# A depthwise convolution of 31 taps: one channel tile on TensorE as diagonal products, or two as 32x32 products

## The chip, the cores and the metric

The kernel runs on one core of one Trainium2 chip. The metric is the device time of one execution in microseconds (us); the median of three runs stands for a kernel. On the core five engines work side by side, each through its own queue in order: TensorE (PE: products; PEld: its weight loads), VectorE (DVE), ScalarE (ACT), GpSimd (POOL) and SyncE (SP, which issues the DMA transfers). TensorE multiplies a stationary block, contracted over up to 128 partitions, with a moving block and adds into banks of PSUM, 128 partitions by 512 values of f32; the other engines read these banks out.

## What is computed

Two layers of a decoder over 256 positions of 1024 channels. Layer 0 has attention and a feed-forward part, layer 1 a gated mixer with a convolution, and again a feed-forward part. The change lies in the convolution of layer 1:

```python
def odd_mixer(h, w_in, b_in, w_out, ln_g, ln_b, w_s, b_s, conv_w, conv_b, cln_g, cln_b):
    proj = h @ w_in + b_in
    gz, ca, cg = jnp.split(proj, [2 * GMLP_WIDTH, 2 * GMLP_WIDTH + CONV_CH], axis=-1)
    gu, gv = jnp.split(jax.nn.gelu(gz), 2, axis=-1)
    ...
    c_out = gu * sg.reshape(B, S, GMLP_WIDTH)
    c = ca * jax.nn.sigmoid(cg)
    c = lax.conv_general_dilated(c, conv_w[:, None, :], window_strides=(1,),
                                 padding=[(CONV_KERNEL - 1, 0)], ...
                                 feature_group_count=CONV_CH) + conv_b
    d_out = jax.nn.silu(layer_norm(c, cln_g, cln_b))
    return jnp.concatenate([c_out, d_out], axis=-1) @ w_out
```

The convolution is depthwise: each of 512 channels has 31 weights of its own, and its output at a position is the weighted sum of the channel at that position and the 30 before it. `sg` is a causal product over blocks of 128 positions, the gate of the other half of the mixer.

## The kernel before, in words

All large products run on TensorE in a split form: an operand is kept as a rounded part (hi) and a remainder (lo), both of type FR, and a product is three passes, hi by hi, lo by hi and hi by lo (`passes`, L222 to L228). Weights come in blocks of 1 MB through three load buffers; ScalarE makes hi (L131), VectorE or GpSimd makes lo (L135), into eight buffers each. These splits are put into a list and taken from it at every `PACE`-th tick, a tick being counted for each 256 columns of a product (L180 to L187).

TensorE's order is the order of the code. GpSimd's is too in the stretch of the change (`pool_order`, L1137), and VectorE's from L1241 on. ScalarE's order, and VectorE's before L1241, are set by a scheduler that may move an operation ahead of others that come before it in the code; on the chip each engine then works its queue strictly in that order.

In layer 1, channels lie on partitions and positions along the row; there are four channel tiles (ct) of 128. The order on TensorE is:

1. `gated(0)`, half of gv, `gated(1)` (L1091): the products for `ca` and `cg`; ScalarE takes the sigmoid, VectorE writes the gated channels with 30 zeros ahead into `cpad`.
2. `project_gu(0)` (L1112), 12 taps of the convolution of tile 3, `project_gu(1)`.
3. The gate, `spatial(p)` for p = 0 to 3 (L1122), with two taps of tile 3 behind each: four small f32 products on 64 columns of the array; ScalarE copies the result out (L1131), GpSimd adds and multiplies (L1132, L1133), ScalarE rounds (L1134), GpSimd takes the remainder (L1135).
4. The other 11 taps of tile 3.
5. The output projection (`out_steps`, L1213), 16 steps of three passes of 512 columns, into four banks taken at that point. Between the steps, in the numbers of `SOME`, stand the small products of the layer norm: `mean` (L1170), the variance (L1188), the scale (L1198). Behind the 16 steps follow those on the convolution's own outputs, which need the norm's result.

Tile 3 is convolved on TensorE (`taps_pe`, L1056): a tap is a product with a diagonal matrix that holds the tap's weight of each channel. A diagonal exists in hi and lo, so a tap is three passes of 256 columns. The 62 diagonals are made by ScalarE from the identity (`tap_diag`, L926), 24 of them in layer 0's feed-forward part and 38 in stage 1. Tiles 0 to 2 are convolved on VectorE (`tap_dve`, L1068): a tap is one operation that multiplies a shifted row of `cpad` with a weight and adds an accumulator in PSUM (`cacc`). These are issued with the ticks, `TAP_RATE` of one per tick, and what is left behind the last product.

Products take a bank from a pool of four (`mm_bank`), used in turn. `tq` in this stretch is a single bank, and `cacc` three more, one for each tile that VectorE convolves.

## Time and profile before

| what | us |
|---|---|
| median of three runs | 617.0 (616.12 to 617.19) |
| the profiled execution's own time | 616.31 |
| its span, first to last instruction | 614.6 |
| TensorE busy in the span | 600.3 (98%) |
| VectorE busy | 409.7 (67%) |
| ScalarE busy | 345.9 (56%) |
| GpSimd busy | 96.7 (16%) |

The rows that follow behind the change are from this one execution. Times in a row are us from the start of the span. In an order of time the columns are: start, duration, engine, line, operation, tile written <- tiles read, shape, count; in square brackets the idle time before it and who ended it. A product's duration includes its way through the array, so products overlap in the rows; the pace is the distance of their starts. A product of two f32 operands shows as two passes.

### The profile page before, as it was taken

How to read it: one execution, taken by the hardware profiler on the slowest of the kernel's cores; microseconds unless marked ns; L12 is line 12 of the kernel's file. 1: busy time of each engine (PE TensorE's matmuls, PEld its weight loads, DVE VectorE, ACT ScalarE, POOL GpSimd, SP SyncE). 2: the span in 40 equal slices, each digit the busy share in tenths (PEclk: the TensorE clock that was granted, in tenths of full speed). 3: DMA queues.
4: the chain of work that ended last, by engine and by line, in shares of the span. 5: the costliest groups of instructions: out<-in, count | busy, mean ns of one | idle time of the engine just before them, and what ended most of it. 6: DMA issues, size and time to landing. Idle time of an engine off the chain costs nothing. (4 is left out here: it accounts for less than half of the span.)

```text
span 614.6 us, 8908 instructions
## 1 busy us (share of the span) xinstructions
PE 600.3 (98%) x3420; PEld 512.3 (83%) x3420; DVE 409.7 (67%) x716; ACT 345.9 (56%) x623; POOL 96.7 (16%) x89
## 2 busy tenths in 40 slices
PE   7989999999999999999999999999999999999997
PEld 5867777788888888888886999878988888888886
DVE  3799998648666648664447499877667666664421
ACT  5766768646555596653346955475555556554310
POOL 1951221001000000000004495541000000000000
PEclk9999999999999999999999999999999999999999
DMA  7947216226766527555563463145665556455301
GB/s 243 328 174 272 71 67 206 69 69 207 258 209 185 189 91 274 206 182 176 193 203 102 139 232 130 51 151 182 218 204 185 167 197 206 166 179 204 138 0 69
DMA packets 72791, 104.32 MB, mean 170 GB/s; under 512 B 3068, under 2 KB 56492, under 8 KB 72748
## 3 DMA queue, kind: packets, MB, share of 16 engines
q1 hardware_dynamic: 72748, 103.74, 50.5%
q8 instruction: 27, 0.44, 0.3%
q14 instruction: 16, 0.13, 0.1%
HBM read 102.69 MB, written 1.05 MB: 169 GB/s over the span
## 5 line engine op out<-in xcount | busy, mean ns | idle before, releaser
L131 ACT ACTIVATE whi<-raw 128x1024 fp32r<-128x1024 f32 (+1 forms) x192 | 197.6, 1041 | 175.4 <-PE mm L233 79.4
L135 DVE TENSOR_TENSOR wlo<-raw,whi 128x1024 fp32r<-128x1024 f32 (+1 forms) x174 | 210.1, 1213 | 123.4 <-ACT whi L131 121.8
L233 PE MATMUL mm<-xT,whi 128*128 128x512 f32 x640 | 226.0, 398 | 0.0
L234 PE MATMUL mm<-xT,wlo 128*128 128x256 f32 x640 | 179.6, 281 | 0.0
L233 PEld LDWEIGHTS mm<-xT,whi 128*128 128x128 f32 x640 | 120.1, 188 | 28.9 <-issue 0.2
L234 PEld LDWEIGHTS mm<-xT,wlo 128*128 128x128 f32 x640 | 120.9, 189 | 0.0
L227 PE MATMUL mm<-whi,hT_lo 128*128 128x512 f32 (+1 forms) x176 | 66.5, 378 | 0.0
L226 PE MATMUL mm<-wlo,hT_hi 128*128 128x512 f32 (+1 forms) x176 | 66.5, 378 | 0.0
L225 PE MATMUL mm<-whi,xT 128*128 128x512 f32 (+1 forms) x176 | 66.0, 375 | 0.4 <-ACT xT L545 0.4
L225 PE MATMUL mm<-whi,hT_hi 128*128 128x512 f32 (+1 forms) x176 | 66.4, 377 | 0.0
L227 PE MATMUL mm<-whi,xT 128*128 128x512 f32 (+1 forms) x176 | 63.0, 358 | 1.2 <-DVE xT L240 1.1
L226 PE MATMUL mm<-wlo,xT 128*128 128x512 f32 (+1 forms) x176 | 62.6, 355 | 0.0
L135 POOL TENSOR_TENSOR wlo<-raw,whi 128x1024 fp32r<-128x1024 f32 (+1 forms) x18 | 41.3, 2331 | 21.9 <-ACT whi L131 21.9
L227 PEld LDWEIGHTS mm<-whi,xT 128*128 128x128 f32 x176 | 33.6, 191 | 7.1 <-DVE xT L240 2.0
L225 PEld LDWEIGHTS mm<-whi,xT 128*128 128x128 f32 x176 | 33.6, 191 | 6.9 <-issue 1.3
L225 PEld LDWEIGHTS mm<-whi,hT_hi 128*128 128x128 f32 x176 | 33.1, 188 | 6.4
L226 PEld LDWEIGHTS mm<-wlo,hT_hi 128*128 128x128 f32 x176 | 33.1, 188 | 6.4
L227 PEld LDWEIGHTS mm<-whi,hT_lo 128*128 128x128 f32 x176 | 33.1, 188 | 6.3
L310 POOL TENSOR_TENSOR rm<-st,neg_half 128x1 f32<-128x1 f32 x8 | 8.0, 1002 | 186.1 <-DVE st L308 186.1
L464 DVE TENSOR_TENSOR scr<-mm,scr 128x256 f32<-128x256 f32 x80 | 33.2, 417 | 5.7 <-ACT scr L463 5.7
L226 PEld LDWEIGHTS mm<-wlo,xT 128*128 128x128 f32 x176 | 33.7, 192 | 3.8 <-DVE wlo L135 0.2
L1077 DVE SCALAR_TENSOR_TENSOR cv<-cpad,cw,cv 128x256 f32<-128x256 f32 x87 | 35.8, 479 | 0.3
(226 smaller groups left out, 843.3 us busy)
## 6 DMA issues: line engine op xcount, KB each, us to landing
raw<-in_ffn_w_in SPq DMA_DIRECT2D x44, 1024.0 KB
raw<-in_ffn_w_out SPq DMA_DIRECT2D x22, 1024.0 KB
raw<-in_even_w_in SPq DMA_DIRECT2D x10, 1024.0 KB
raw<-in_odd_w_in SPq DMA_DIRECT2D x8, 1024.0 KB
raw<-in_even_w_out SPq DMA_DIRECT2D x4, 1024.0 KB
raw<-in_odd_w_out SPq DMA_DIRECT2D x4, 1024.0 KB
xs<-in_x SPq DMA_DIRECT2D x4, 256.0 KB
raw<-in_even_w_in SPq DMA_DIRECT2D x4, 256.0 KB
```

The source lines that it names most:

```text
L131: nc.scalar.activation(self.half(f)[0][:, r], self.source(f)[:, r], AF.Copy)
L135: self.lo_engine[f].tensor_tensor(lo[:, r], self.source(f)[:, r], hi[:, r].bitcast(F32), op=ALU.subtract)
L225: nc.tensor.matmul(ps, lhs[0], rhs[0], start=first, stop=False)
L226: nc.tensor.matmul(ps, lhs[0], rhs[1], start=False, stop=False)
L227: nc.tensor.matmul(ps, lhs[1], rhs[0], start=False, stop=last)
L233: nc.tensor.matmul(bank, w[0], x[2][:, k, :, :].rearrange("p a b -> p (a b)"), start=k == 0, stop=False)
L234: nc.tensor.matmul(bank[:, :S], w[1], x[0][:, k, :], start=False, stop=k == KT - 1)
L310: nc.gpsimd.tensor_tensor(r, t[:, 1:2], neg_half[:, :1], op=ALU.pow)
L464: nc.vector.tensor_tensor(s, bank[:, :S], s, op=ALU.add)
L1077: nc.vector.scalar_tensor_tensor(conv[:, ct, :] if t == TAPS - 1 else acc, cpad[:, ct, t:t + S], cw[:, t, ct:ct + 1], acc, op0=ALU.mult, o ...
```

## The change

Tiles 2 and 3 are convolved on TensorE, tiles 0 and 1 on VectorE. The products are f32, not split, and have no diagonals of 128: the channels are taken in four groups of 32 partitions (r), the taps in four classes (c, the tap's number modulo 4). A product takes 32 rows and 32 columns of the array: its stationary block is the diagonal of one tap for one group (`W32`, made by GpSimd from `same`, four identities of 32 stacked), its moving block the shifted row of `cpad`. Group r adds into bank r, class c into partitions 32c to 32c + 31 of it. So sixteen products have sixteen places of the array and sixteen places of PSUM. The four banks are copied to SBUF (`evacuate`: two by ScalarE, two by VectorE), and a last product with `same` adds the four classes and puts each group on its own partitions (`fold`, into `cacc[2]`); VectorE adds the bias.

The diagonals, the rounded weights for them (`cw2`, `cw_hi`) and the split of tile 3 (`c_hi`, `c_lo`) go away. The taps stand in two parts: behind the gate's first two blocks tile 2, behind the other two tile 3; the 12 taps ahead of `project_gu(1)` and those between the gate's blocks are gone. The gate's odd blocks use `cacc[2]` instead of a bank of the pool. Two output steps, the fold and two more steps stand ahead of the mean, instead of three steps. `TAP_RATE` is 0.65.

```diff
--- before.py
+++ after.py
@@ -61,9 +61,9 @@
 N_T1 = (10, 5, 10)
 
 
-TAP_RATE = 0.55
-N_DIAG = 12
-SOME = (3, 4, 1, 2, 1)
+ON_PE = (2, 3)
+TAP_RATE = 0.65
+SOME = (2, 4, 1, 2, 1)
 LAMBDA_INIT = 0.8 - 0.6 * math.exp(-0.3 * 0)
 
 
@@ -918,15 +918,11 @@
     wsT = mp.tile([P, NH, P], F32, name="wsT")
     biasT = mp.tile([P, 4, P], F32, name="biasT")
     cw = mp.tile([P, TAPS, 4], F32, name="cw")
-    cw2 = mp.tile([P, 2, TAPS * 4], F32, name="cw2")
     bv = mp.tile([P, 512], F32, name="bv")
     ones = mp.tile([P, P], F32, name="ones")
-    diag = mp.tile([P, N_DIAG, 2, P], FR, name="diag")
-
-    def tap_diag(d, t, ct):
-
-        for i in range(2):
-            nc.scalar.activation(d[:, i, :], ident, AF.Copy, scale=cw2[:, i, t * 4 + ct:t * 4 + ct + 1])
+
+    same = mp.tile([P, 32], F32, name="same")
+    W32 = {ct: mp.tile([P, TAPS, 32], F32, name=f"W32_{ct}") for ct in ON_PE}
 
     def odd_setup(ptag):
 
@@ -977,12 +973,10 @@
         nc.tensor.transpose(pt[:, :TAPS * 4], cw_rows[:TAPS * 4, :P], ident[:TAPS * 4, :TAPS * 4])
         cwf = cw.rearrange("p a b -> p (a b)")
         nc.vector.tensor_copy(cwf, pt[:, :TAPS * 4])
-        hi = mp.tile([P, TAPS * 4], FR, name="cw_hi")
-        nc.scalar.activation(hi, cwf, AF.Copy)
-        nc.vector.tensor_copy(cw2[:, 0, :], hi.bitcast(F32))
-        nc.vector.tensor_tensor(cw2[:, 1, :], cwf, hi.bitcast(F32), op=ALU.subtract)
-        for t in range(N_DIAG):
-            tap_diag(diag[:, t], t, 3)
+        nc.vector.tensor_reduce(same, ident.rearrange("p (a b) -> p b a", b=32), axis=AX.X, op=ALU.add)
+        for ct in ON_PE:
+            nc.gpsimd.tensor_tensor(W32[ct], same[:, None, :].to_broadcast([P, TAPS, 32]),
+                                    cw[:, :, ct, None].to_broadcast([P, TAPS, 32]), op=ALU.mult)
         yield
 
     with tc.tile_pool(name="ffn0", bufs=1) as fp, tc.tile_pool(name="pf0", bufs=1, space=bass.MemoryType.PSUM) as pf:
@@ -1050,18 +1044,41 @@
         cpad = op.tile([P, 4, S + TAPS - 1], F32, name="cpad")
         nc.gpsimd.memset(cpad[:, :, :TAPS - 1], 0.0)
         conv = op.tile([P, 4, S], F32, name="conv")
-        c_hi = op.tile([P, S + TAPS - 1], FR, name="c_hi")
-        c_lo = op.tile([P, S + TAPS - 1], FR, name="c_lo")
-
-        def taps_pe(ct):
-
-            ps = mm_bank()
-            for t in range(TAPS):
-                d = diag[:, t] if t < N_DIAG else diag2[:, t - N_DIAG]
-                passes(ps[:, :S], (d[:, 0, :], d[:, 1, :]), (c_hi[:, t:t + S], c_lo[:, t:t + S]), t == 0, t == TAPS - 1)
-                if t < TAPS - 1:
-                    yield
-            nc.vector.tensor_scalar(conv[:, ct, :], ps[:, :S], col("conv_b", ct), None, op0=ALU.add)
+
+        class ConvPE:
+
+
+
+            def __init__(self):
+                self.banks = [mm_bank() for _ in range(4)]
+
+            def taps(self, i):
+                cs = slice(i * S, (i + 1) * S)
+                ct = ON_PE[i]
+                for t0 in range(0, TAPS, 4):
+                    for r in range(4):
+                        rs = slice(32 * r, 32 * r + 32)
+                        for c in range(min(4, TAPS - t0)):
+                            t = t0 + c
+                            nc.tensor.matmul(self.banks[r][32 * c:32 * c + 32, cs], W32[ct][rs, t, :], cpad[rs, ct, t:t + S],
+                                             start=t0 == 0, stop=t + 4 >= TAPS)
+                    tick(1)
+
+            def evacuate(self):
+                self.parts = [scratch() for _ in range(4)]
+                for r in range(4):
+                    if r % 2:
+                        nc.vector.tensor_copy(self.parts[r], self.banks[r])
+                    else:
+                        nc.scalar.activation(self.parts[r], self.banks[r], AF.Copy)
+
+            def fold(self):
+                ps = cacc[2]
+                for i, ct in enumerate(ON_PE):
+                    cs = slice(i * S, (i + 1) * S)
+                    for r in range(4):
+                        nc.tensor.matmul(ps[32 * r:32 * r + 32, cs], same, self.parts[r][:, cs], start=True, stop=True)
+                    nc.vector.tensor_scalar(conv[:, ct, :], ps[:, cs], col("conv_b", ct), None, op0=ALU.add)
 
         live, credit = deque(), [0.0]
 
@@ -1100,9 +1117,7 @@
                     sigmoid = nc.scalar.activation(sgm, ps[:, :S], AF.Sigmoid, bias=col("b_in", 12 + ct))
                     nc.vector.scalar_tensor_tensor(cpad[:, ct, TAPS - 1:], ps[:, S:], col("b_in", 8 + ct), sgm,
                                                    op0=ALU.add, op1=ALU.mult)
-                    if ct == 3:
-                        split(c_hi, c_lo, cpad[:, ct, :])
-                    else:
+                    if ct not in ON_PE:
                         live.append((ct, 0))
             return sigmoid
 
@@ -1120,7 +1135,7 @@
             return gelu
 
         def spatial(p):
-            pg = mm_bank() if p % 2 else tq()
+            pg = cacc[2] if p % 2 else tq()
             for c in range(MT):
                 for h in range(2):
                     g = 2 * p + h
@@ -1136,29 +1151,24 @@
 
         pool_order = in_order("Pool")
         gated(0)
-        diag2 = op.tile([P, TAPS - N_DIAG, 2, P], FR, name="diag2")
-        for t in range(N_DIAG, TAPS):
-            tap_diag(diag2[:, t - N_DIAG], t, 3)
         run(gv_steps(1))
         last = gated(1)
         with tc.issue_after(last.ins):
             for m in range(MT):
                 gv_stats(m)
         project_gu(0)
-        taps = taps_pe(3)
-        for _ in range(N_DIAG):
-            next(taps)
         for m in range(MT):
             gv_norm(m)
         last = project_gu(1)
         with tc.issue_after(last.ins):
 
             nc.scalar.activation(small.tile([P, 2], F32, name="st2")[:, 0:1], ident[:, 0:1], AF.Silu)
-        for p in range(4):
-            spatial(p)
-            for _ in range(2):
-                next(taps)
-        run(taps)
+        conv_pe = ConvPE()
+        for i in range(2):
+            for p in (2 * i, 2 * i + 1):
+                spatial(p)
+            conv_pe.taps(i)
+        conv_pe.evacuate()
         while live:
             tap_dve()
         background.clear()
@@ -1168,7 +1178,7 @@
         cm = [None] * MT
 
         def mean():
-            for i, ct in enumerate((3, 0, 1, 2)):
+            for i, ct in enumerate((0, 1, 2, 3)):
                 nc.tensor.matmul(pm[:, :S], ones, conv[:, ct, :], start=i == 0, stop=i == 3)
 
         def center(m):
@@ -1240,6 +1250,8 @@
 
         order = in_order("DVE")
         some(SOME[0])
+        conv_pe.fold()
+        some(2)
         mean()
         low(late[0], 0)
         low(late[1], 0)
```

## Rows read from the trace of the kernel before

**Rows 1.** The page: busy time of TensorE; the span in 40 slices, clock and GpSimd.

```profile
PE 600.3 (98%) x3420; PEld 512.3 (83%) x3420; DVE 409.7 (67%) x716; ACT 345.9 (56%) x623; POOL 96.7 (16%) x89
...
POOL 1951221001000000000004495541000000000000
PEclk9999999999999999999999999999999999999999
```

**Rows 2.** Windows: busy time of each engine in the stretch of the convolution's products.

```profile
374.80:395.60 20.80, 20.11 (x176) 18.81 (x175) 19.75 (x48) 8.64 (x15) 11.50 (x12) 1.00 0.18 58
```

**Rows 3.** TensorE in order of time, from the taps to the mean.

```profile
374.88 0.28 PE L225 MATMUL mm<-c_hi,diag 128*128 128x256 f32 x1
...
379.14 0.28 PE L225 MATMUL mm<-xT,whi 128*128 128x256 f32 x1
...
384.79 0.28 PE L227 MATMUL mm<-xT,wlo 128*128 128x256 f32 x1
...
385.81 0.28 PE L226 MATMUL mm<-c_lo,diag 128*128 128x256 f32 x1
...
388.75 0.66 PE L1127 MATMUL tq<-wsT,gn 128*64 128x128 f32 x8 [0.69 <-ACT scr L1131]
...
395.49 0.28 PE L227 MATMUL mm<-c_hi,diag 128*128 128x256 f32 x1
395.61 0.40 PE L225 MATMUL mm<-whi,oT_hi 128*128 128x512 f32 x1
...
397.67 1.89 PE L1172 MATMUL tq<-conv,ones 128*128 128x256 f32 x8
```

**Rows 4.** VectorE's taps in order of time; ScalarE's copies for the diagonals (source line).

```profile
379.39 15.36 DVE L1077 SCALAR_TENSOR_TENSOR cv<-cpad,cw,cv 128x256 f32<-128x256 f32 x39
...
L929 ACT ACTIVATE diag<-ident,cw x62: 385/389/403, 217.8 to 354.1; 128x128 fp32r<-128x128 f32 x62
```

**Rows 5.** TensorE in order of time: products on parts of the array.

```profile
89.31 0.37 PE L700 MATMUL tq<-T_dk,T_dq 32*128 32x256 f32 x1
89.31 0.37 PE L700 MATMUL mm<-T_dk,T_dq 32*128 32x256 f32 x1
89.52 0.37 PE L700 MATMUL tq<-T_dk,T_dq 32*128 32x256 f32 x1
...
202.51 1.09 PE L968 MATMUL tq<-wsT,ones 128*64 128x128 f32 x16
```

**Rows 6.** ScalarE in order of time, from gu to the gate.

```profile
385.05 1.06 ACT L131 ACTIVATE whi<-raw 128x1024 fp32r<-128x1024 f32 x1 [1.83 <-PE mm L226]
386.01 0.82 ACT L1118 ACTIVATE guT<-mm,vec 128x256 f32<-128x256 f32 x2
...
390.36 0.42 ACT L1134 ACTIVATE oT_hi<-scr 128x256 fp32r<-128x256 f32 x1 [0.43 <-POOL scr L1133]
```

**Rows 7.** ScalarE's copies out of a bank (source line).

```profile
L239 ACT ACTIVATE xT<-cv x4: 576/590/599, 339.0 to 422.9; 128x512 fp32r<-128x512 f32 x4
```

**Rows 8.** GpSimd in order of time, two tiles of the gate.

```profile
388.77 0.73 POOL L1132 TENSOR_TENSOR scr<-scr,biasT 128x256 f32<-128x256 f32 x1 [7.05 <-ACT scr L1131]
...
391.55 0.73 POOL L1132 TENSOR_TENSOR scr<-scr,biasT 128x256 f32<-128x256 f32 x1
```

**Rows 9.** End of the output steps: VectorE and TensorE in order of time.

```profile
409.67 0.68 DVE L240 TENSOR_TENSOR oT_lo<-scr,oT_hi 128x512 fp32r<-128x512 f32 x1
...
410.46 0.44 PE L227 MATMUL mm<-whi,oT_lo 128*128 128x512 f32 x1
```

**Rows 10.** TensorE's first products in order of time.

```profile
8.30 0.63 PE L225 MATMUL mm<-whi,xT 128*128 128x512 f32 x1
8.72 0.63 PE L226 MATMUL mm<-wlo,xT 128*128 128x512 f32 x1
...
11.69 0.39 PE L226 MATMUL mm<-wlo,xT 128*128 128x512 f32 x1
11.92 0.39 PE L227 MATMUL mm<-whi,xT 128*128 128x512 f32 x1
```

## The prediction

> **What bounds the kernel now.** I read the page first: TensorE is busy for 98% of the span, so only time taken off or put on TensorE's own queue can count [rows 1]. Then the table by stretches: in the 20.8 us that hold the convolution's products TensorE is busy for 20.1, while VectorE, with 19.8, is also nearly full [rows 2]. Which of the two ends last is seen in TensorE's order of time: the last of the products, at 395.49, is followed at once by the first output step at 395.61, and the mean's products at 397.67 follow three such steps without a gap [rows 3]. So VectorE's 31 taps of each tile, one every 0.39 us (15.36 us for 39), end just in time and TensorE sets the pace [rows 4]. What VectorE is spared (one tile, 31 x 0.39 = 12 us) and what ScalarE is spared (62 copies of 0.39 us each for the diagonals) lies beside TensorE's work and brings nothing by itself [rows 4].
>
> **What the stretch costs before.** From the first product at 374.88 to the output steps at 395.61 it takes 20.73 us [rows 3]. The first 12 taps are 36 products in 374.88 to 379.14, 0.119 each; 31 taps are 93 products, 11.0 us. The second half of gu is 48 products, 5.8 us. The four blocks of the spatial gate make up the rest: around the first, the product after next starts 1.02 us after the one before (384.79 to 385.81) where two paces would be 0.24, so a block costs 0.78. Of this 0.43 is streaming (8 passes at 0.054, below) and 0.35 the two changes of tile shape, 0.17 each. The third block also waits 0.7 us for ScalarE (388.75). Sum: 11.0 + 5.8 + 3.1 + 0.8 = 20.7.
>
> **What it costs after.** A product of two f32 operands is two passes of 256 columns, 0.21 to 0.22 us each [rows 5]. The change has 124 products of 32x32 per tile (31 taps x 4 groups), 248 in all, 496 passes. Whether sixteen run at once no row shows. Two do: in the attention, products on two groups of 32 rows start within 0.01 us of each other and the next two 0.21 later, each pair as long as a single one; and two halves of 64 columns do it for longer: 16 passes of 128 columns take 1.09 us where 8 take 0.66, (1.09 - 0.66)/8 = 0.054 per pass [rows 3, 5]. The bounds are therefore 16 rounds x 0.43 = 6.9 us, if all sixteen overlap, and 496 x 0.054 = 26.8 us, if passes come no faster than the fastest that the trace sustains. I take 6.9: in the rows at 89.31 the second product starts at once, so it is the array that spaces them, not the issuing, and the f32 passes leave 13 ns for each of 32 passes in a round.
>
> Nothing of this has to be loaded while it runs except weights of 32 columns, beside the streaming. Changes of tile shape in this stretch: gu to gate, gate to 32x32, back, again, and to the output steps, five, 0.85 us. Gate blocks: 4 x 0.43 = 1.7. One wait is new at the start: the four banks are those of the last four tiles of that pool, and the fourth is gu's second, which ScalarE frees. Before, gu ends at 384.9 and ScalarE first does a weight split (385.05), then both gelus (386.01 to 386.83) [rows 6]. So the fourth group can start 1.9 us after gu, while two gate blocks fill 1.2 of it: 0.7 lost. The wait of the third block is gone, since sixteen-at-once work stands before it. Sum: 5.8 + 1.7 + 6.9 + 0.85 + 0.7 = 16.0, so the last pass ends at about 390.9.
>
> **The copies out of the banks.** The output steps use the same four banks, so TensorE now stands still until a bank is copied out. The first copy is ScalarE's, 0.59 us by the nearest row of that size [rows 7], with hand-over about 0.9. If it came at once, the steps would start at 391.8. But ScalarE works its queue in order: the gelus of 386.01 stood behind a split that had to wait [rows 6]. The four gate tiles each have a copy on ScalarE that waits for two GpSimd operations, and in the code they come before the copies out. GpSimd takes 2.78 us per tile (388.77 to 391.55) and sets that chain [rows 8]; it starts 4.3 us earlier than before, as gu does (12 taps of 36 products no longer lie ahead), at 384.5. The fourth tile's copy comes 3 x 2.78 + 1.6 later (the first, at 390.36, was 1.6 behind the start), at 394.4, and takes 0.4 [rows 6, 8]. A copy out behind it ends at 395.5, so the steps start at 395.6: where they start before. This is my choice: the code's order, and a queue that I have seen block.
>
> **After that.** The last products (fold) are two rounds of four, 0.86, and two changes of shape, 0.34: 1.2 us on the path. VectorE's two additions of the bias, of a tap's size (0.39 each), lie beside the two output steps that follow, 1.4 us, and the mean of the other tiles. Before the mean there are four steps now instead of three, so one fewer (0.68 us) stands behind it to cover the normalisation. That cover has no slack: VectorE's low part of the first half ends at 410.35 and the TensorE product that reads it starts at 410.46 [rows 9]. So 0.7 more. Off the path: the 32-wide weights on GpSimd, by its 0.73 us for 256 columns about 2.9 us per tile [rows 8], in a stretch where GpSimd's row of the page shows zeros [rows 1]; VectorE's two copies out; fewer ticks (16 for 31), since gu's ticks have emptied the list of splits before and the late ones are issued by hand. If GpSimd had no such free stretch, 5.8 us would come onto its queue, long before the weights are read.
>
> **The sum.** 0.0 for the start of the steps, + 1.2 + 0.7 = +1.9 us. The profiled execution took 616.3 us (span 614.6 and 1.7 around it), so 618.2; it lay 0.7 below the median of 617.0, so on the median 618.9.
>
> **One rule against the change.** The rows at 89.31 show products 0.01 us apart on two row groups [rows 5], which says nothing of 496 in a row. The Trainium skill, TensorEngine Tiling (Array Packing), Instruction Overhead, counts about 60 cycles for each matmul, 25 ns at 2.4 GHz. By that the passes would take an estimated 12.4 us instead of 6.9; two starts 10 ns apart or less speak against it as a spacing between tiles, none against it over a long stream.
>
> **Rivals.**
> *The copies out are not held up* (0.36). ScalarE's order is not the code's throughout: the split of 385.05, which the code has behind the convolution (L1232), runs before the gelus [rows 6]. If the copies stand ahead of the third and fourth gate tile, the steps start at 391.8, 3.8 us earlier, and 3.8 - 1.2 - 0.7 = 1.9 us are won: 615.0. This is the side of faster; it decides at products under 8.1 us (up to there over 0.2% remains).
> *Issuing bounds the products* (0.13). Between the bounds of 0.0134 and 0.054 us per pass the geometric middle is 0.027, 13.3 us in all: the passes end 6.4 later than in the rival above, so +4.5, 621.5, whatever ScalarE does. The skill's figure, named above, would give 620.5.
> *Passes at the fastest sustained pace* (0.10): 26.8 us, 19.9 more than 6.9 and so +18.0, 634.9.
> *It doesn't run sixteen at once* (0.03), but two, as far as the rows go: 248 x 0.43 / 2 = 53 us, 661.
>
> The forecast has 0.38. It has a cost of its own that I leave out of the sum: TensorE would stand still for 4.6 us. At the start of the kernel products of 512 columns come every 0.43 us (8.30, 8.72) against 0.23 at 395.61, half the rate; that is 1.2 against 2.4 GHz by columns per time, though the page's clock row says full [rows 1, 3, 10]. It was over by 11.69 (0.23 to the next), so worth up to half of 3.4, 1.7 us; whether this pause brings it, no row says. It would make 620.6.
>
> **How the numbers follow.** A measurement here tells about 0.2%, 1.2 us, from no change. Faster by more: the first rival with products under 8.1 us, 0.30. Within: the rest of that rival 0.06, forecasts that come out a little lower 0.08, slower issue with a quick copy 0.01: 0.15. Slower: 0.55. The range, 614.6 to 623.5, holds the forecast with its clock loss, the first rival, and issuing up to 15 us; it leaves out the last two rivals and a little at both ends, under 0.2. The forecast's own range is 617.5 to 621.5.
>
> **What would show it.** Right: rounds of 16 products 0.43 us apart; TensorE idle for some 4 us before the first output step, ended by ScalarE's copy out, which stands right behind the fourth gate tile's copy; the fold in 1.2 us; a wait of about 0.7 at the end of the output steps. Wrong: copies out directly behind the last pass (615), rounds of 0.8 us or more (621 and up), or a stretch between 375 and 396 in which something else that I hold for covered, VectorE's taps or GpSimd's splits, ends last.

## The result, and the profile after

The changed kernel takes 622.64 us in the median of five runs (621.84 to 623.32); the kernel before took 617.19 beside it. The ratio is 1.009, with an interval of 1.0075 to 1.0104: 5.4 us slower, where +1.9 was forecast. The profiled execution took 622.17 us, its span is 620.4 against 614.6. The median is inside the range and on the side that had the larger chance, but 3.7 us above the forecast, and the parts of the sum show why. One execution of a later variant (975.4 us, at a granted clock of 0.56) is in none of the ratios below.

The page of the kernel after: TensorE is busier by 3.0 us and the span longer by 5.8.

```profile
span 620.4 us, 9664 instructions
...
PE 603.3 (97%) x3839; PEld 507.9 (82%) x3839; DVE 400.9 (65%) x686; ACT 329.2 (53%) x561; POOL 100.6 (16%) x91
```

TensorE of the kernel after in order of time, the rows that answer to [rows 3]: gu's second half, the 32x32 products (L1063), the first output step, the fold (L1080), the mean (L1182), a product of the variance (L1201), and the product that waits for the late low half [rows 9].

```profile
377.00 0.28 PE L225 MATMUL mm<-xT,whi 128*128 128x256 f32 x1
...
383.87 0.69 PE L1063 MATMUL mm<-cpad,W 32*32 32x256 f32 x24
384.74 4.66 PE L1063 MATMUL mm<-cpad,W 32*32 32x256 f32 x224 [0.18 <-ACT guT L1133]
...
390.35 0.65 PE L1063 MATMUL mm<-cpad,W 32*32 32x256 f32 x12
391.50 2.76 PE L1063 MATMUL mm<-cpad,W 32*32 32x256 f32 x128 [0.50 <-issue]
394.95 2.59 PE L1063 MATMUL mm<-cpad,W 32*32 32x256 f32 x108 [0.69 <-issue]
397.72 0.50 PE L225 MATMUL mm<-whi,oT_hi 128*128 128x512 f32 x1 [0.17 <-ACT scr L1073]
...
399.31 0.64 PE L1080 MATMUL cv<-scr,same 128*32 128x256 f32 x8
400.69 0.64 PE L1080 MATMUL cv<-scr,same 128*32 128x256 f32 x8 [0.73 <-DVE conv L1081]
...
402.76 1.89 PE L1182 MATMUL tq<-conv,ones 128*128 128x256 f32 x8
...
408.90 0.38 PE L1201 MATMUL tq<-ones,scr 128*128 128x1 f32 x2 [0.36 <-DVE ms L298]
...
416.00 0.51 PE L227 MATMUL mm<-whi,oT_lo 128*128 128x512 f32 x1 [0.38 <-DVE oT_lo L240]
```

Four marks cut the kernel into parts that can be compared. They are the first product behind gu's first half (before 374.88, after 377.00), the first output step (395.61, 397.72), the first product of the mean (397.67, 402.76), and the product that waits for the late low half (410.46, 416.00). The last column counts the fourth output step (0.7), which moved from behind the mean to ahead of it, by itself.

| part | before | after | forecast of the difference | measured |
|---|---|---|---|---|
| up to the stretch | 374.88 | 377.00 | 0 | +2.1 |
| stretch, to the first step | 20.73 | 20.72 | 0.0 | 0.0 |
| first step to mean | 2.06 (3 steps) | 5.04 (4 steps) | 1.2 + one step | 2.3 + one step (0.7) |
| mean to late product | 12.79 | 13.24 | one step less, 0.7 lost | one step less, 1.1 lost |
| behind it, to the end | 204.1 | 204.4 | 0 | +0.3 |

2.1 + 0.0 + 2.3 + 1.1 + 0.3 = 5.8. So one of the surprises lies 50 to 140 us ahead of the edit, the fold cost twice its price, and the stretch itself came out at the forecast number. The last is partly luck: within it the products took far longer than forecast. Their group by line, after (busy, mean ns, then idle time ahead):

```profile
L1063 PE MATMUL mm<-cpad,W 32*32 32x256 f32 x496 | 11.3, 385 | 1.4 <-issue 1.2 <-ACT guT L1133 0.2
```

11.3 + 1.4 = 12.7 us, where 6.9 of products and 0.7 of bank wait were forecast: 5.1 too little. Over the row of 224 passes they start 0.019 apart on average ((4.66 - 0.39) / 223), not 0.0134, and twice the row stops with the reason "issue". The beginning of that row runs at the forecast pace. Windows of these products alone, at its head (busy time and count of PE, then of PEld):

```profile
384.74:384.86 0.12, 0.12 (x16) 0.12 (x29) 1.00 0.00 0
384.74:385.20 0.46, 0.46 (x33) 0.35 (x34) 1.00 0.00 0
```

Sixteen passes start within 0.12 us, and a single one streams for 0.21 [rows 5], so the sixteen places do work at once; 33 passes start in 0.46 us, a round of 32 in little more than the 0.43 of the forecast. Behind this first round a round takes 32 x 0.019 = 0.61 us.

ScalarE and VectorE in order of time, after: the gate's fourth rounding copy (L1149), then the four copies out (L1073, L1071).

```profile
396.48 0.42 ACT L1149 ACTIVATE oT_hi<-scr 128x256 fp32r<-128x256 f32 x1 [2.33 <-POOL scr L1148]
397.07 1.09 ACT L1073 ACTIVATE scr<-mm 128x512 f32<-128x512 f32 x2 [0.17 <-PE mm L1063]
...
397.14 1.29 DVE L1071 COPY scr<-mm 128x512 f32<-128x512 f32 x2 [10.82 <-PE mm L1063]
```

ScalarE's queue frees itself at 396.90 (396.48 + 0.42) and the products release the copies 0.17 later. The gate's chain came out as forecast: its fourth rounding copy starts at 394.4 if the 2.1 us that arose ahead of the stretch are taken off. Two chains that were forecast 3.8 us apart (steps at 391.8 by the products, at 395.6 by the gate's copies) now end together, which is why the start of the steps did not move. VectorE stands idle for 10.8 us ahead of its copy: what it was spared was worth nothing, as forecast.

### The profile page after: what moved, and what is told of

Same layout as the page of the kernel before. It is cut to its first block, busy times and chain, and to the rows that moved or that the text cites. A ratio compares the mean times of both kernels' runs of the same rounds, so it can differ in the third digit from the quotient of the medians.

```text
span 620.4 us, 9664 instructions
## 1 busy us (share of the span) xinstructions
PE 603.3 (97%) x3839; PEld 507.9 (82%) x3839; DVE 400.9 (65%) x686; ACT 329.2 (53%) x561; POOL 100.6 (16%) x91
## 5 line engine op out<-in xcount | busy, mean ns | idle before, releaser
L135 DVE TENSOR_TENSOR wlo<-raw,whi 128x1024 fp32r<-128x1024 f32 (+1 forms) x174 | 212.7, 1228 | 129.8 <-ACT whi L131 129.1
L463 ACT ACTIVATE scr<-mm 128x256 f32<-128x256 f32 x80 | 29.3, 366 | 0.1
```

The source lines that it names most:

```text
L135: self.lo_engine[f].tensor_tensor(lo[:, r], self.source(f)[:, r], hi[:, r].bitcast(F32), op=ALU.subtract)
L463: nc.scalar.activation(s, bank[:, S:], AF.Copy)
```

## The experiments

Marks as above; "stretch" is always from the first product behind gu's first half to the first output step. The kernel before, run again, comes first; it had no edit.

> The kernel before, unchanged, profiled once more. In the changed kernel's profile TensorE's passes of 512 columns come every 236 and 231 ns between 228 and 330 us (layer 0's feed-forward part, long before the convolution), where the profile of before has 230 and 227: 2.1 of the 5.8 us by which its span is longer. If that pace belongs to the kernel, this profile has 230 and 227 there again and a span of 614.6 within 0.5. If it is a matter of the single execution, one of two such profiles may well have 236 and a span near 617.

It took 618.16 us, span 616.3, 1.7 more than the first profile. TensorE's pace in layer 0's feed-forward part explains a part of it (0.8 us, by the distance of the same products in both profiles): its first half (236 to 266 us) had 172 products in 30 us where the first profile of the same kernel had 175. The second half (292 to 322) had 134 in both.

### What bounds the products: the array or the issuing

The moving block of every product but the first and last round of taps is halved, so that these taps cover half of the positions.

```diff
-                            nc.tensor.matmul(self.banks[r][32 * c:32 * c + 32, cs], W32[ct][rs, t, :], cpad[rs, ct, t:t + S],
-                                             start=t0 == 0, stop=t + 4 >= TAPS)
+                            n = S if t0 == 0 or t + 4 >= TAPS else S // 2
+                            nc.tensor.matmul(self.banks[r][32 * c:32 * c + 32, i * S:i * S + n], W32[ct][rs, t, :],
+                                             cpad[rs, ct, t:t + n], start=t0 == 0, stop=t + 4 >= TAPS)
```

> The changed kernel, but the 32x32 products of all rounds except the first and last of each tile move 128 columns instead of 256 (half of the positions of tiles 2 and 3 lack taps 4 to 27). Theory (TensorE's issuing of many short instructions sets the pace, about 16.7 ns per pass in the long runs of the profile, whatever a pass moves): the products keep their length, 12.4 us for both tiles with their waits, within 0.5, and the time stays at 622.2 within 1. Rival (the sixteen places of the array, or their reads and writes, set the pace): rounds of half the width take half as long, 3 to 4 us off the products, 618 to 619.5.

624.5 us in one execution: not faster, and 1.9 above the changed kernel, so neither forecast met the time. TensorE in order of time, and its windows (the clock is the third figure from the end):

```profile
385.73 3.88 PE L1064 MATMUL mm<-cpad,W 32*32 32x256 f32 x224 [0.17 <-ACT guT L1134]
...
392.49 2.33 PE L1064 MATMUL mm<-cpad,W 32*32 32x256 f32 x128 [1.28 <-issue]
395.94 3.28 PE L1064 MATMUL mm<-cpad,W 32*32 32x128 f32 x108 [1.13 <-issue]
```

```profile
393.00:396.00 3.00, 1.87 (x115) 1.32 (x107) 0.00 (x0) 0.49 (x2) 2.40 (x5) 0.71 0.02 5
396.00:399.00 3.00, 3.00 (x108) 1.91 (x108) 0.00 (x0) 0.89 (x2) 2.40 (x4) 0.50 0.02 5
```

At full clock the 224 passes start 0.016 apart ((3.88 - 0.29) / 223) instead of 0.019. Half the columns save a sixth of the spacing, where they would have halved it if the streaming in the array set the pace. So the larger part is a cost of each pass, whatever it moves. Whether this is the issuing itself or the weight load that each pass brings along (496 of 0.10 us each, overlapping) no run separates; below, "issuing" stands for both. The granted clock fell from 1.00 to 0.50, the lower of the two levels, at 394.3, between the two stops, and the last 108 passes ran at 0.50. With stops 1.2 longer in all, and 1.0 us that arose ahead of the stretch, this gave back what the narrower blocks had saved.

The stops named "issue" have a place of their own. Counted from the first 32x32 pass, they come in the kernel after behind pass 260 (24 + 224 + 12) and 128 passes later; in the run above and the run of the next section at the same two. 128 passes with their weight loads are 256 instructions. The DMA queues of the kernel after between 383 and 400 us (the first line is the rate in 40 slices of 0.425 us):

```profile
GB/s 0 0 0 39 0 0 65 133 320 383 388 388 388 335 106 0 0 0 0 0 0 0 39 0 0 0 0 0 0 0 39 0 0 0 0 0 0 0 0 39
...
q8 instruction: 5, 0.08, 2.2%
```

Five transfers of 16 KB of instructions start at 384.3, 389.0 (hidden in the row by a load of weights), 392.6, 396.1 and 399.8, so 3.4 to 3.8 us apart in the stretch of the stops. TensorE goes on at 391.50 and 394.95, each time 2.3 to 2.5 us behind the start of a transfer. This holds in every run of this document: all 17 stops named "issue" in the stretch end 2.3 to 2.6 us behind the start of such a transfer, though they last from 0.2 to 1.3 us, and the next transfer starts 1.1 us behind the end of the stop (1.6 in three cases). That TensorE runs out of instructions and waits for the next transfer fits the places, the transfers and this distance; that the transfers are the cause was argued from this and not tried by itself. The length of the stops varies, 1.2 us in all in the kernel after, 2.4 and 2.0 in these two runs.

### The fold

All eight products of the fold run ahead of VectorE's two additions, instead of four, an addition, four.

```diff
                     for r in range(4):
                         nc.tensor.matmul(ps[32 * r:32 * r + 32, cs], same, self.parts[r][:, cs], start=True, stop=True)
+                for i, ct in enumerate(ON_PE):
+                    cs = slice(i * S, (i + 1) * S)
                     nc.vector.tensor_scalar(conv[:, ct, :], ps[:, cs], col("conv_b", ct), None, op0=ALU.add)
```

> The changed kernel with the eight products of the fold first and VectorE's two additions behind them. Theory: the 0.73 us that TensorE's fifth to eighth product of the fold waits for VectorE's first addition goes, and the kernel is 0.4 to 0.8 us faster than the changed one, 621.8 to 622.2 on its median of 622.6. Rival (the mean behind it waits for the additions anyway): the wait moves to the mean's products, no difference over 0.2.

622.77 us (621.54 to 624.18), ratio 1.0088 (1.0059 to 1.0118): no difference that the times show. But the trace (TensorE in order of time) has the saving in its place:

```profile
392.05 2.76 PE L1063 MATMUL mm<-cpad,W 32*32 32x256 f32 x128 [0.74 <-issue]
396.05 2.59 PE L1063 MATMUL mm<-cpad,W 32*32 32x256 f32 x108 [1.24 <-issue]
398.81 0.50 PE L225 MATMUL mm<-whi,oT_hi 128*128 128x512 f32 x1 [0.17 <-ACT scr L1073]
400.41 1.07 PE L1080 MATMUL cv<-scr,same 128*32 128x256 f32 x16
402.92 1.89 PE L1184 MATMUL tq<-conv,ones 128*128 128x256 f32 x8
```

From the first step to the mean it is 4.10 instead of 5.04: the fold costs 1.3 with its step taken off (4.10 - 2.06 - 0.70), which is the 1.2 of the forecast. The 0.7 that the kernel after loses there is the second half of the fold, which writes the tile that VectorE's addition of the first half still reads. In this profile the two stops were longer by 0.8 and took the gain back (stretch 21.50 instead of 20.72): here the transfers started 1.6 us behind the last stop's end instead of 1.1. Whether they do so in every execution of this kernel stays open.

### The products spread out

Tile 2's products stand ahead of gu's second half, tile 3's in two parts behind the first and second gate block; the last two gate blocks behind all of them.

```diff
+        conv_pe = ConvPE()
+        conv_pe.taps(0)
         for m in range(MT):
             gv_norm(m)
         last = project_gu(1)
...
+        spatial(0)
+        conv_pe.taps(1, range(0, 16, 4))
+        spatial(1)
+        conv_pe.taps(1, range(16, TAPS, 4))
+        for p in (2, 3):
+            spatial(p)
         conv_pe.evacuate()
```

> The changed kernel with the same products in three parts that are not next to each other: tile 2 between the two halves of gu, tile 3 in two parts of four rounds around the gate's second block; gu then uses two other banks, and the gate's last two blocks follow the products. Theory (the two waits of 0.9 and 1.1 us inside tile 3's products, which the profile names issue, are TensorE waiting for its own instructions to be fetched, about one fetch of 256 instructions in 3.4 us): with gu's 96 long instructions in between, most of the 2.0 us goes, the wait of 0.55 for gu's bank goes too, and one or two more changes of shape cost 0.2 to 0.35 each: 1.5 to 2.3 us faster than the changed kernel, 620.3 to 621.1, if the gate's later last blocks delay nothing. Rival (the waits come from the products themselves, their banks or places): they stay, and the time is within 0.7 of 622.6.

624.16 us (623.74 to 625.23), ratio 1.0116: slower. The stops named "issue" fell only from 1.2 to 0.9 us in all, where the theory had most of them go, and TensorE now stood still at the end:

```profile
398.90 0.50 PE L225 MATMUL mm<-whi,oT_hi 128*128 128x512 f32 x1 [1.76 <-ACT scr L1073]
```

The gate starts some 6 us later with gu (389.1, against 382.85 in the kernel after), so its copies on ScalarE are late and hold up the copies out: the second chain of the stretch became the longer one. The theory had named such a delay by the last gate blocks as its condition.

### The chain on ScalarE

Most of tile 3's products are left out, so that they end some 5 us earlier. First with the copies out in their place behind the gate's fourth copy, then with all four on VectorE, which is idle.

```diff
-                for t0 in range(0, TAPS, 4):
+                for t0 in range(0, TAPS if i == 0 else 4, 4):
...
-                spatial(p)
+                last = spatial(p)
             conv_pe.taps(i)
-        conv_pe.evacuate()
+        with tc.issue_after(last.ins):
+            conv_pe.evacuate()
```

> The changed kernel without most of tile 3: of its 31 taps only the first 4 are done on TensorE (32 of 248 passes), so 27 taps of that tile are missing from the result. The four copies out of the banks stay where they are on ScalarE and VectorE, behind the gate's fourth rounding copy on ScalarE (in the changed kernel at 396.48). Theory (ScalarE's queue holds the copies out, so that the products' length alone didn't decide when the output steps start): the products end at about 391, TensorE then stands still for 6 us, the steps start at 397.5 to 397.9 as in the changed kernel, and the time is the same: 621.9 to 622.8. Rival (the products alone set the end): 216 passes of 0.025 us are gone, 5.4 us, time about 617.

626.18 us in one execution. TensorE in order of time, ScalarE's copies, and windows of the three us behind the standstill:

```profile
380.08 0.28 PE L225 MATMUL mm<-xT,whi 128*128 128x256 f32 x1
...
394.58 0.68 PE L1063 MATMUL mm<-cpad,W 32*32 32x256 f32 x20 [0.51 <-issue]
400.45 0.80 PE L225 MATMUL mm<-whi,oT_hi 128*128 128x512 f32 x1 [5.18 <-ACT scr L1073]
```

```profile
399.49 0.42 ACT L1149 ACTIVATE oT_hi<-scr 128x256 fp32r<-128x256 f32 x1 [2.31 <-POOL scr L1148]
399.82 1.06 ACT L1073 ACTIVATE scr<-mm 128x512 f32<-128x512 f32 x2
```

```profile
400.00:403.00 3.00, 2.55 (x6) 1.82 (x6) 0.00 (x0) 0.88 (x2) 3.00 (x2) 0.50 0.00 0
```

216 passes fewer, and the stretch is 20.37 instead of 20.72: the copies out wait for ScalarE's queue, as the forecast said they would with short products. TensorE stands still for 5.2 us. The time is above what was expected for two reasons outside of that: this execution reached the stretch 3.1 us later than the kernel after (380.08 against 377.00; the clock was 0.59 from 342 to 346 us), and the granted clock, which fell 1.3 us into the standstill, was still 0.50 for three us behind it, so that from the first step to the mean it took 6.31 instead of 5.04.

> As the run before (27 taps of tile 3 missing from the result), but all four copies out are VectorE's, which has nothing else to do then. Theory: the steps start some 0.9 us behind the last pass, at 392 to 392.5; the fourth copy ends 2.6 us behind the last pass, which can delay the fold by about 0.7; time 622.2 - 5.4 + 0.7 = 617 to 618. Rival (something else than ScalarE's queue holds the steps, such as the gate's own outputs): 621 or more.

618.52 us in one execution, 0.5 above the forecast, with the stretch reached 1.6 later than in the kernel after. TensorE in order of time:

```profile
378.63 0.28 PE L225 MATMUL mm<-xT,whi 128*128 128x256 f32 x1
...
393.13 0.68 PE L1063 MATMUL mm<-cpad,W 32*32 32x256 f32 x20 [0.51 <-issue]
393.75 0.50 PE L225 MATMUL mm<-whi,oT_hi 128*128 128x512 f32 x1
```

Stretch 15.1: 5.3 us less for the same products, by moving two copies to another queue. The two runs together show that the stretch of the changed kernel has two ends, the products and the gate's copies on ScalarE, and that shorter products bring next to nothing (0.35) while the copies stay. The other half, the copies on VectorE with products of full length, was not run; that it brings little follows from the rows of the kernel after, where the products themselves release the copies only at 397.07 and 397.14.

### The pace of layer 0

The tables of the change are 5712 bytes per partition smaller than those that it removes, so the operands hT_hi and hT_lo of layer 0's feed-forward part lie elsewhere. An unused tile puts them back.

```diff
     same = mp.tile([P, 32], F32, name="same")
+    pad = mp.tile([P, 1428], F32, name="pad")
```

> The changed kernel with 5712 bytes per partition left unused among the small tables, which puts the operands hT_hi and hT_lo of layer 0's feed-forward part back to the SBUF addresses that they have in the kernel before (174272 and 196800 instead of 168544 and 191072). Theory (the pace of that part's second half, 227 ns per pass of 512 columns in both profiles of the kernel before and 231 to 233 in all four of the changed kernel and its variants, goes with where its operands lie): 227 again, 1.6 us less, 621.0. Rival (it goes with something else, or is chance): 231 to 233 and 622.6.

620.4 us (618.41 to 621.18), ratio 1.0082 (1.006 to 1.0104). Windows of the second half, 30 us in each: before, after, and with the old addresses.

```profile
292.00:322.00 30.00, 30.00 (x134) 24.86 (x133) 14.42 (x12) 12.19 (x12) 0.00 (x0) 1.00 0.59 202
```

```profile
292.00:322.00 30.00, 30.00 (x130) 24.14 (x129) 12.80 (x11) 11.92 (x12) 0.00 (x0) 1.00 0.57 197
```

```profile
292.00:322.00 30.00, 30.00 (x134) 24.82 (x133) 13.60 (x12) 12.74 (x12) 0.00 (x0) 1.00 0.59 208
```

134, 130, 134 products of the same shape: 227 ns apart, then 231 or 232 with every third one 237 or 238, then 227. The slower pace stood in all eight profiles of a kernel with the changed addresses, the faster in all six with the old. It is worth some 1.6 us (the shift against the kernel before grows from 0.4 at 273 us to 2.0 at 326); the ratio moved in that direction by less than its interval, so the times do not show it by themselves. Why these addresses cost some 6 ns per product was not found, nor whether it is hT's place alone: the unused tile moves all that is allocated behind it. This one profile is also short at its end (202.3 us behind the late product instead of 204.4). Of the later runs one without the unused tile shows the same and two with it do not, so this is not the tile's doing. The first half's pace changes between executions of one kernel (the first run above) and is chance here.

The changed kernel once more, without an edit:

> The changed kernel again, for its spread. Theory: the waits named issue come at the same places in the stream of products (behind the 260th and the 388th pass) with other lengths, since the place goes with the instructions' addresses and the length with when their transfer starts; the second half of layer 0's feed-forward part runs at 231 to 233 ns per pass of 512 columns again; ratio to the kernel before 1.007 to 1.011. Rival (both are chance of the one profile): other places, 227.

623.01 us (622.52 to 623.91), ratio 1.0109 (1.0081 to 1.0137), as expected. Stops behind pass 260 and 388 again, stretch 20.59, first step to mean 5.05, mean to late product 13.24, and 130 products in the window above.

### Sharing a tile

VectorE idles for 10.8 us, TensorE is short of time: 19 taps of tile 2 go back to VectorE, and all copies out with them (344 passes instead of 496).

```diff
+PE_TAPS = (12, 31)
+N2 = 12
...
-                for t0 in range(0, TAPS, 4):
+                n = PE_TAPS[i]
+                for t0 in range(0, n, 4):
...
-                    if ct not in ON_PE:
-                        live.append((ct, 0))
+                    if ct < 3:
+                        live.append((ct, 0 if ct < 2 else N2))
```

> Tile 3 and the first 12 taps of tile 2 as 32x32 products on TensorE (344 passes instead of 496), the other 19 taps of tile 2 on VectorE in its idle 10.8 us (19 x 0.39 = 7.5), all copies out by VectorE, both halves of the fold ahead of the additions, three output steps ahead of the fold and one behind. Theory (passes cost 0.025 each all told, and nothing else holds the steps once VectorE copies): 152 x 0.025 = 3.8 us less, fold 0.9 less: about 618 against 622.6. Rival (VectorE, now with 81 taps and four copies, ends last): 621 or more.

Ratio 1.0086 (1.0055 to 1.0116), median 621.93 beside 615.19. The rival was right: VectorE ends last.

```profile
389.13 5.20 DVE L1099 SCALAR_TENSOR_TENSOR cv<-cpad,cw,cv 128x256 f32<-128x256 f32 x10
...
395.16 2.48 DVE L1073 COPY scr<-mm 128x512 f32<-128x512 f32 x4
```

```profile
394.00:396.00 2.00, 0.01 (x1) 0.04 (x1) 1.97 (x5) 0.28 (x1) 1.56 (x3) 1.00 0.00 0
396.00:398.00 2.00, 2.00 (x7) 1.61 (x8) 1.64 (x3) 0.42 (x1) 1.47 (x3) 0.78 0.00 0
398.00:400.00 2.00, 2.00 (x12) 0.80 (x15) 0.00 (x0) 0.00 (x0) 2.00 (x1) 0.50 0.00 0
```

Ten of its last taps, all into one bank of PSUM, take 0.52 each instead of 0.39, TensorE stands still for 2.3 us, and the clock falls to 0.50 behind that. The next two versions move tile 2's sums to another bank (`cacc[2]`), put two copies on ScalarE ahead of the gate's fourth (`finish` issues that one), and use the old addresses.

```diff
-            acc = cacc[ct][:, :S] if ct < 2 else cacc[0][:, S:]
+            acc = cacc[ct][:, :S] if ct < 2 else cacc[2][:, S:]
...
+        last = conv_pe.evacuate()
+        with tc.issue_after(last.ins):
+            finish()
```

> As the run with the shared tile (tile 3 and 12 taps of tile 2 as 32x32 products, 19 taps of tile 2 on VectorE), mended where it lost: tile 2's sums on VectorE in a bank of their own and taken in turn with the others (0.39 a tap instead of 0.52), two of the copies out on ScalarE ahead of the gate's fourth rounding copy, the fold behind two output steps and one step behind it, hT_hi and hT_lo at their old addresses. Theory: TensorE never stands still for more than about 1 us between the last product and the first step, so the granted clock stays at 1.00; the steps start some 3 us earlier, by the distance to gu, than in the kernel before, of which the fold takes 1.2 and a wait at the end nothing, since the norm starts earlier: about 1.5 to 2 us faster than the kernel before, ratio 0.997. Rival (the stretch behind the steps' start is held by the norm's chain, whatever TensorE does before): ratio 1.00 or more.

618.43 us (616.55 to 620.09), ratio 1.0029 (1.0011 to 1.0047): the time is the rival's, not the theory's, but for another reason than the rival's, which follows below.

> As the run with early copies, with 16 instead of 12 taps of tile 2 on TensorE: 32 passes more, 0.5 to 0.8 us, and 4 taps less on VectorE, 1.6 us. Theory (with 12 taps the two engines end at about the same time): TensorE ends last and the time is 0.3 to 0.8 above that of the run with 12. Rival (VectorE still ends last with 12): faster than with 12 by up to 1 us.

619.72 us (618.46 to 621.19), ratio 1.0051 (1.0031 to 1.0071): 1.3 above, more than expected. The two intervals overlap, so that 12 is the better number is likely and not certain. Both had a new wait (2.3 and 2.7 us), shown for 12 taps in TensorE's order of time and windows:

```profile
383.96 1.12 PE L1148 MATMUL cv<-wsT,gn 128*64 128x128 f32 x8 [2.31 <-DVE cv L1100]
```

```profile
384.00:387.00 3.00, 3.00 (x74) 1.93 (x76) 3.00 (x9) 1.43 (x4) 1.78 (x3) 0.50 0.84 261
387.00:390.00 3.00, 3.00 (x63) 2.09 (x46) 2.77 (x8) 0.86 (x2) 2.40 (x4) 0.50 0.28 94
```

`cacc[2]` is not tile 2's alone: the gate's second block writes the other half of it, and waits for VectorE's taps. Six us at half the clock follow (three with 16 taps). The last version gives the gate a single bank and sets its four blocks apart.

```diff
-            pg = cacc[2] if p % 2 else tq()
+            pg = tq()
...
+        spatial(0)
+        conv_pe.taps(0, range(0, PE_TAPS[0], 4))
+        spatial(1)
+        conv_pe.taps(1, range(0, 16, 4))
+        spatial(2)
+        conv_pe.taps(1, range(16, TAPS, 4))
+        last = conv_pe.evacuate()
+        with tc.issue_after(last.ins):
+            spatial(3)
```

> As the run with early copies and 12 shared taps, but all four gate blocks use the one bank of their own, so that none of them waits for VectorE's sums, and they stand apart: the first ahead of the products, the second behind tile 2's, the third in the middle of tile 3's, the fourth behind the last product, where it covers the copies out. Theory: the 2.3 us that the second gate block waited for VectorE's taps, and the half clock of some 3 us behind it, are gone; two more changes of tile shape (0.3) and the waits named issue (0.3 to 0.9) come back: some 3 us less than that run, ratio to the kernel before 0.996 to 0.999. Rival (something behind the start of the output steps, the norm's chain or the gate's last tile, which is now 2 us later, ends last): 1.00 to 1.003.

615.27 us (613.16 to 616.69) beside 616.63: ratio 0.9973, interval 0.9958 to 0.9988, as forecast. It is faster than both kernels, than the kernel before by 0.3%. TensorE in order of time:

```profile
376.03 0.28 PE L226 MATMUL mm<-xT,whi 128*128 128x256 f32 x1
...
391.12 1.96 PE L1066 MATMUL mm<-cpad,W 32*32 32x256 f32 x76 [0.29 <-issue]
393.01 0.66 PE L1147 MATMUL tq<-wsT,gn 128*64 128x128 f32 x8
393.71 0.50 PE L226 MATMUL mm<-whi,oT_hi 128*128 128x512 f32 x1
395.30 1.07 PE L1084 MATMUL cv<-scr,same 128*32 128x256 f32 x16
397.10 1.89 PE L1191 MATMUL tq<-conv,ones 128*128 128x256 f32 x8
```

The stretch is 17.7, the fold costs 1.3, and the norm's chain starts 1.7 earlier in relation to the stretch: 17.68 + 3.39 = 21.07 against 20.73 + 2.06 = 22.79.

## Why the prediction was right and wrong

- **The sign and the range** held: slower, at 622.6 in 614.6 to 623.5. The forecast's own range, 617.5 to 621.5, did not.
- **The products, 6.9 us, failed.** The step was "it is the array that spaces them, not the issuing", read from two products that start 0.01 apart [rows 5]. Two starts show how near two instructions can follow each other, not how many a long row of them gets: at the head of a row 33 passes do start in 0.46 us, and behind that the pace is lost. Measured: 0.019 per pass over a row, of which halving the columns saved 0.003, and two stops; 12.7 us with the bank wait. The Trainium skill, TensorEngine Tiling (Array Packing), Instruction Overhead, counts about 60 cycles for each matmul, 25 ns at 2.4 GHz, by which I had estimated 12.4. That sum came much nearer, but in part by chance: the spacing in a row is below those 25 ns, and the rest are stops. The rival on issuing had the nearer size, 13.3 us, and its mechanism, a cost of each pass, is borne out by the halved columns as far as that run goes; its time of 621.5 came near by luck, since the longer products did not move the steps.
- **The start of the steps, 0.0, held** (20.72 against 20.73), and its mechanism, ScalarE's queue in the code's order, was shown with short products: with 216 passes fewer the stretch shrank by 0.35, and by 5.6 once VectorE copied. But because the products were longer by 5.1, TensorE did not stand still for 4.6 us; it waited 0.17. The error and the slack cancelled, and that the number held is luck. The clock that a standstill would have cost, left out of the sum with "up to 1.7", is 1.3 in the run that had it.
- **The fold, 1.2, was right for its products and missed a wait.** 1.3 when its halves follow each other, 2.3 as written, because the second half writes a tile that VectorE is still reading. I had put both additions beside the output steps.
- **The tail, 0.7, came out at 1.1.** There is a second wait beside the one that I had named: 0.36 us of idle time at the second variance product (408.90), and 0.38 at the late product (416.00). From the mean to the late product it is 13.24 in all profiles with four steps ahead of the mean (13.20 to 13.25) and 12.8 in those with three: with four steps this chain has no slack, as said, and every delay of the mean reached the late product in full.
- **Nothing in the sum stood for layer 0** (+2.1). I counted what the edit removes and adds there on the other engines, but not that freeing tables moves operands. About 1.6 of it goes with the addresses, the rest with the first half's pace, which is chance: 175 products in 30 us in the first profile of the kernel before, 171 to 173 in all the others.
- **Signs and slips.** Of the signs named for being right, the order on ScalarE and a wait at the end appeared; rounds of 0.43 us and a standstill of 4 us did not. In the working, the first rival's bound of 8.1 us of products should be 7.6 (1.9 - 1.2 = 0.7 above 6.9), and the third gate block's wait of 0.7 stands in the first sum as 0.8; neither changes the forecast.
- The relief of VectorE and ScalarE brought nothing, and GpSimd's work on `W32` (busy 100.6 us against 96.7) cost nothing, as forecast. The bank wait is 0.4 instead of 0.7: the 25th pass starts 0.87 behind the first, where 24 at 0.019 take 0.46.

## What to carry over

Before splitting one product into hundreds of small ones, price a long row of instructions, not a pair, and count the instructions: 496 passes cost 12.7 us here, although at the pace of a row's first 33 (0.46 us) they would have taken 6.9. When a wait looks covered, name the second chain that ends at nearly the same time, and look at both before mending one: the version that won shares the work with the idle engine, takes the copies out of a blocked queue, and never lets TensorE stand still for more than half a microsecond. After any change to what is allocated, compare the pace of identical products far from the edit.

## What the runs showed of the hardware

- Sixteen 32x32 products ran at once at the head of a row (33 passes started in 0.46 us). In a long row the passes came 0.019 us apart, 0.016 with half the columns, so that most of the spacing did not go with what a pass moves.
- A long row of short products stops at fixed places, 128 passes (256 instructions) apart, for 0.2 to 1.3 us of idle time. All 17 stops ended 2.3 to 2.6 us behind the start of an instruction transfer of 16 KB.
- Products of 512 columns ran at 227 or at 231 to 238 ns with two placements of the tiles in SBUF, in 14 profiles without an exception.
- VectorE's tap took 0.39 us when two or three banks were used in turn, 0.52 when ten in a row used one.
- The granted clock fell to 0.50 in or behind standstills of 2.3 us (two runs), 2.7 us (16 shared taps) and 5.2 us, for some three to seven us; one of 1.8 us, in the run with the products spread out, left it at 1.00. The length of a single standstill does not decide it: a standstill of 1.55 us at some 338 us is in all 14 profiles, and the clock fell in or behind it in three of them; and with half the columns it fell behind a stop of 1.3 us.
